# A two-layer hybrid encoder step: the FFN's down projection with the contraction outermost, Strassen operand sums two tiles at a time on VectorE

## The chip, the cores and the metric

One core of a Trainium2 chip. The metric is the device time of one execution in microseconds: the median of the runs, 3462.66 us before the change.

## What is computed

A two-layer encoder step in float32: per layer an RMSNorm, one input projection into four head groups (latent attention, RWKV-7, Mamba-2, gated DeltaNet), an output projection with residual, then RMSNorm and a gated convolutional FFN with residual; a final RMSNorm. The change lies between the output projection and the next layer:

```python
x = x + mix @ P['w_out'][l]
u, new_hist = _dwconv(_rmsnorm(x, g2) @ w_up, hist, conv_w)   # 1024 -> 2 x 2816
gate, val = jnp.split(u, 2, axis=-1)
x = x + (jax.nn.silu(gate) * val) @ w_down                    # 2816 -> 1024
```

The activations lie transposed: 1024 features are eight tiles (`KD`) of 128 partitions, and the 1076 positions (prompt, meta tokens and samples) are three blocks of 308, 384 and 384 columns (`XBLK`). The FFN's 2816 inner features are 22 tiles (`NFF`).

## The kernel before

Every large product is made in a split form: an operand is stored as a rounded high part and the remainder as a low part (`split`, line 277: the high part is a copy on ScalarE, the low part a subtraction on VectorE, or on GpSimd where `pool` is set), and `dense` (line 298) adds three matmuls for each tile of the contraction: high by high, high by low, low by high. `load_w` (line 286) loads a weight tile of up to 1024 columns into one of two raw buffers (`wraw`) and splits it into one of two pairs (`whi`, `wlo`).

The program is written in order of the work, and a scheduler orders each engine's instructions by priority: program order, with the stretches under `high_priority` moved ahead. PSUM has eight buffers of a bank, under tags: two `d`, two `g`, one each of `c`, `h`, `e`, `i` (line 1897). All DMAs are issued by SyncE (`dma`, line 262), in its order.

**Output projection and norm (`w_out`, line 1494).** For each block, eight output tiles `ops` are made, added to the residual tile `xt[b][m]` on VectorE (line 1534) and written to HBM. Then `norm2` squares the eight tiles on ScalarE, adds them up in two accumulators (on VectorE and GpSimd, in block 2 on VectorE alone), sums over the partitions by two matmuls with ones into `nps` (tag `g`, lines 324 to 326) and gets the factor by Ln and Exp. Block 0's and block 1's normed tiles are split into `h0` and `h1` (half of the low parts on GpSimd).

**Strassen operands (lines 1553 to 1575).** Blocks 1 and 2 together go through the up projection as a two by two product with seven products. Its sums of normed tiles are made one 384-column tile at a time: `a11 - a21`, `a22 - a11` and the low parts of S2, S1, S3, S4 on VectorE, the sums `a21 + a22` (line 1567), `a12 - s2` (line 1572) and the low parts of A22 on GpSimd. The seven products of each of the 22 inner tiles (`up12`, line 1658; tile `upq`) need them; block 0 (`up0`, line 1639; tile `ups`) needs only `h0`. `ffn_w` (line 1585) loads two weight tiles, splits them and makes Strassen's four weight sums on GpSimd, in two steps around a `yield`.

**Down projection (lines 1702 to 1744).** The gated tiles lie in HBM (`gd`). `gates(b)` loads a block's 22 tiles as eleven pairs `gr` and splits them into `gh`, `gl` (twelve buffers each). Then each of eight output tiles takes its whole contraction:

```python
for m in range(KD):
    ps = self.pp.tile([P, 512], F32, tag="dg"[m % 2], name=self.nm("wps"))
    for k0 in range(0, NFF, KD):
        kk = min(KD, NFF - k0)
        c = (m % 4 * NFF + k0) * P
        w = self.load_w(io["wdnl"][l, m // 4][:, c:c + kk * P], kk * P)
        self.dense(ps[:, :n], w, xs[k0:k0 + kk], 0, n, 0, k0 == 0, k0 + kk == NFF)
    self.tt(xt[m], xt[m], ps[:, :n], ALU.add)
```

So one output tile needs all 22 gated tiles and three weight tiles (1024, 1024, 768 columns). After the third output tile (`m == 2`) of blocks 1 and 2 the norm of the block before is written (`f(b - 1, prev)`: in layer 0 the next layer's first norm, in layer 1 `out_block`, the final norm and the output). The last block's comes after the loop.

Of the kernel before, what the change touches and what calls it, by code (L numbers as in the profile page):

```python
# [8 lines left out]
F32 = mybir.dt.float32  # L9
# [7 lines left out]
P = 128  # L17
DM = 1024
KD = 8
# [13 lines left out]
NSLOT = 17  # L33
DFF = 2816
NFF = 22
FG = [(0, NFF)]
NF = 5
TI = 800
RB = 0.4
# [159 lines left out]
class Net:  # L199
# [86 lines left out]
    def load_w(self, src, n=1024, act_hi=True, pool=None):  # L286
        raw = self.wp.tile([P, 1024], F32, tag="wraw", name=self.nm("wraw"))
        if pool is None:
            hi = self.wp.tile([P, 1024], F32R, tag="whi", name=self.nm("whi"))
            lo = self.wp.tile([P, 1024], F32R, tag="wlo", name=self.nm("wlo"))  # L290
        else:
            hi = pool.tile([P, 1024], F32R, tag="g", name=self.nm("gwh"))
            lo = pool.tile([P, 1024], F32R, tag="g", name=self.nm("gwl"))
        self.dma(raw[:, :n], src)
        self.split(hi[:, :n], lo[:, :n], raw[:, :n], act_hi)
        return hi, lo

# [14 lines left out]
    def mean_sq(self, xt, n, adds=None):  # L312

        t = lambda tag: self.sp.tile([P, 384], F32, tag=tag, name=self.nm(tag))
        accs = []
        for e in range(2):
            acc = t("na")
            self.act(acc[:, :n], xt[4 * e], AF.Square)
            accs.append(acc)
            for k in range(4 * e + 1, 4 * e + 4):  # L320
                sq = t("nt")
                self.act(sq[:, :n], xt[k], AF.Square)
                (adds or (self.nc.vector, self.nc.gpsimd)[e]).tensor_tensor(acc[:, :n], acc[:, :n], sq[:, :n], op=ALU.add)
        ps = self.pp.tile([P, 512], F32, tag="g", name=self.nm("nps"))
        for e in range(2):
            self.mm(ps[:, :n], self.cc("ones"), accs[e][:, :n], e == 0, e == 1)
        r = accs[0]
        self.rsqrt(r[:, :n], ps[:, :n], 1.0 / DM, 1, accs[1][:, :n])
        return r
# [18 lines left out]
    def norm2(self, xt, b):  # L348

        n = XBLK[b][1]  # L350
        r = self.mean_sq(xt, n, self.nc.vector if b == 2 else None)
# [1134 lines left out]
    def x_block(self, pool, b, src, tag=None):  # L1486

        c0, n = XBLK[b]
        xt = [pool.tile([P, 308 if tag else 384], F32, tag=tag or f"x{k}", name=self.nm("x"))[:, :n] for k in range(KD)]
        for k in range(KD):  # L1490
            self.dma(xt[k], src[k][:, c0:c0 + n])
        return xt

    def w_out(self, l, xdram):

        sa, sb = SIDES[l % 2], SIDES[1 - l % 2]
        xq = self.new("xq", {f"x{k}": 2 for k in range(KD)}, side=sa)
        fq = self.new("fq", dict(x=KD, y=8, g=4), side=sa)
        xt = {}
        for b in [*range(NFB, NBLK), *range(NFB)]:  # L1500
            part = b >= NFB
# [22 lines left out]
        for b in range(NBLK):  # L1524
            c0, n = XBLK[b]
            if b == 2:
                yd[b] = y_last(b)
                ya[b] = self.y_tiles((0,), b)
            for m in range(KD):
                ps = self.pp.tile([P, 512], F32, tag="dei"[m % 3], name=self.nm("ops"))  # L1530
                w = ws[m // 2]
                self.dense(ps[:, :n], w, ya[b], 0, n, m % 2 * 512, True, False)
                self.dense(ps[:, :n], w, yd[b], 0, n, m % 2 * 512 + 256, False, True)
                self.tt(xt[b][m], xt[b][m], ps[:, :n], ALU.add)
                self.dma(self.xres[m][:, c0:c0 + n], xt[b][m])
            if b == 0:
                self.aq.release()
                self.ap.release()
                self.ha = self.new("ha", dict(h0=16, h1=16), side=sb)
                self.h0 = self.pairs(self.ha, 308, KD, "h0")  # L1540
                self.h1 = self.pairs(self.ha, 384, KD, "h1")
            if b == 2:
                with self.tc.high_priority(HPO):
                    self.fw = self.ffn_w(l, 0)
                    next(self.fw)
            scale = self.norm2(xt[b], b)
            if b < 2:
                for k in range(KD):
                    self.split(*(self.h0, self.h1)[b][k], scale(k), pool=k % 2)
        fq.release()  # L1550


        self.hx = self.new("hx", {f"h{i}": 2 * KH for i in range(5)}, side=sb)
        S2, S1, S3, S4, A22 = self.hm = [self.pairs(self.hx, 384, KH, f"h{i}") for i in range(5)]
        sub = lambda o, a, b: self.tt(o, a, b, ALU.subtract)
        K = range(KH)
        a11, a12, a21, a22 = xt[1][:KH], xt[1][KH:], xt[2][:KH], xt[2][KH:]
        s2 = []
        for k in K:
            scale(k)  # L1560
            scale(KH + k)
            sub(a11[k], a11[k], a21[k])
            s2.append(self.sp.tile([P, 388], F32, tag="s", name=self.nm("s2"))[:, :384])
            sub(s2[k], a22[k], a11[k])
            self.split(*S2[k], s2[k])
        for k in K:
            self.nc.gpsimd.tensor_tensor(a21[k], a21[k], a22[k], op=ALU.add)
            self.split(*S1[k], a21[k])
        for k in K:
            self.split(*S3[k], a11[k])  # L1570
        for k in K:
            self.nc.gpsimd.tensor_tensor(a12[k], a12[k], s2[k], op=ALU.subtract)
            self.split(*S4[k], a12[k])
        for k in K:
            self.split(*A22[k], a22[k], pool=True)
        xq.release()
        self.pw.release()

# [6 lines left out]
    def ffn_w(self, l, j):  # L1585

        raws, ws = [], []
        for i in range(2):
# [3 lines left out]
            self.split(*w, raw)  # L1592
            raws.append(raw)
            ws.append(w)
        (B11, B21), (B12, B22) = ((r[:, 0:512], r[:, 512:1024]) for r in raws)
        g = lambda o, a, b, op: self.nc.gpsimd.tensor_tensor(o, a, b, op=op)
        g(B22, B22, B12, ALU.subtract)
# [13 lines left out]
    def ffn(self, l, after):  # L1611
# [27 lines left out]
        def up0(j):  # L1639

            with self.tc.high_priority(HPO):
                w = self.fw if j == 0 else self.ffn_w(l, j)
                W[j] = [x for x in w if x][0]
# [55 lines left out]
        wt.release()  # L1699
        self.hx.release()  # L1700
        self.ha.release()
        xq = self.new("xe", {f"x{k}": 2 for k in range(KD)}, side=sa)
        gq = self.new("gq", dict(gr=3), side=sa)
        ng = 0

        def gates(b):

            nonlocal ng
            c0, n = XBLK[b]
            out = []  # L1710
            for r in range(NFF // 2):
                raw = gq.tile([P, 2, 384], F32, tag="gr", name=self.nm("gr"))[:, :, :n]
                i = ng % 12
                hi, lo = ((gq if i < 8 else xq).tile([P, 2, 384], F32R, tag=f"{s}{i}", name=self.nm(s))[:, :, :n]
                          for s in ("gh", "gl"))
                ng += 1
                self.dma(raw, gd[2 * r:2 * r + 2][:, :, c0:c0 + n].rearrange("j p n -> p j n"))
                self.split(hi, lo, raw)
                out += [(hi[:, i], lo[:, i]) for i in range(2)]
            return out  # L1720

        prev = None
        for b in range(NBLK):
            n = XBLK[b][1]
            with self.tc.high_priority(HPO):
                xs = gates(b)
            xt = self.x_block(xq, b, self.xres)
            for m in range(KD):
                ps = self.pp.tile([P, 512], F32, tag="dg"[m % 2], name=self.nm("wps"))
                for k0 in range(0, NFF, KD):  # L1730
                    kk = min(KD, NFF - k0)
                    c = (m % 4 * NFF + k0) * P
                    w = self.load_w(io["wdnl"][l, m // 4][:, c:c + kk * P], kk * P)
                    self.dense(ps[:, :n], w, xs[k0:k0 + kk], 0, n, 0, k0 == 0, k0 + kk == NFF)
                self.tt(xt[m], xt[m], ps[:, :n], ALU.add)
                if m == 2 and b == 0:
# [198 lines left out]

    def out_block(self, xt, b):
        c0, n = XBLK[b]
        r = self.mean_sq(xt, n)
        for k in range(KD):
            t = self.sp.tile([P, 388], F32, tag="s", name=self.nm("yt"))  # L1940
            self.stt(t[:, :n], xt[k], self.vec("fin", k), r[:, :n], ALU.mult, ALU.mult)
            self.dma(self.io["o_y"][k][:, c0:c0 + n], t[:, :n])


class MultiPool:
# [141 lines left out]
```

## Time and profile before

| | us |
|---|---|
| runs | 3462.30, 3462.66, 3464.98 (median 3462.66) |
| profiled execution | 3456.34 |
| its span | 3454.3 |
| PE busy | 3274.8 (95%) |
| DVE busy | 2393.8 (69%) |
| ACT busy | 1608.3 (47%) |
| POOL busy | 789.4 (23%) |

PE is TensorE, DVE VectorE, ACT ScalarE, POOL GpSimd, SP SyncE. Busy times are sums over stages with different limits; the PE row counts overlapped matmuls, so a stretch is better read by how many matmuls it holds. In layer 0 the output projection and the Strassen operands end near 1000 us, the up projection near 1450 us, the down projection near 1740 us; in layer 1 near 2720, 3152 and 3442 us.

### The profile page before, as it was taken

To read this page: it belongs to the slowest core of one execution; us is meant where nothing else is said; L and a number is where in the kernel's file an instruction comes from. 1 tells how busy PE (TensorE), PEld (TensorE's weight loads), DVE (VectorE), ACT (ScalarE), POOL (GpSimd) and SP (SyncE) were. 2 spreads that over 40 slices of the span, in tenths; PEclk is the share of its full clock that TensorE was granted. 3 is DMA by queue.
4 is the path that set the end of the run, shared out by engine and by line. 5 is a ranking of instruction groups with operands and counts; after the bars stand their busy time and mean duration, and the time that the engine had idled before them with its cause. 6 is when DMAs were issued, how large, how long until landed. Compare 5 with 4: busy or idle time off the path is not lost. (4 is left out here: it accounts for less than half of the span.)

```text
span 3454.3 us, 66279 instructions
## 1 busy us (share of the span) xinstructions
PE 3274.8 (95%) x25954; PEld 2939.2 (85%) x25954; DVE 2393.8 (69%) x4527; ACT 1608.3 (47%) x3285; POOL 789.4 (23%) x1305
## 2 busy tenths in 40 slices
PE   7999999998889999899999999999988999998998
PEld 6988885776879999889998888767768899998998
DVE  5477774774689999845535778657647899996553
ACT  4455555454444444434335555544544444444432
POOL 3000012000255555300020000120004555551000
PEclk9999998999999999999999999989999999999999
DMA  3222223421412222376532232334132222225664
GB/s 133 87 74 78 71 85 100 118 65 49 153 52 75 75 74 74 117 221 190 161 106 72 70 86 70 99 92 124 45 96 94 68 75 75 75 74 171 191 189 128
DMA packets 267417, 350.20 MB, mean 101 GB/s; under 512 B 75424, under 2 KB 225888, under 8 KB 266976
## 3 DMA queue, kind: packets, MB, share of 16 engines
q1 hardware_dynamic: 267104, 345.96, 32.8%
q8 instruction: 204, 3.34, 0.4%
q14 instruction: 109, 0.89, 0.1%
HBM read 256.17 MB, written 89.71 MB: 100 GB/s over the span
## 5 line engine op out<-in xcount | busy, mean ns | idle before, releaser
L283 DVE TENSOR_TENSOR wlo<-wraw,whi 128x1024 fp32r<-128x1024 f32 (+1 forms) x307 | 362.3, 1181 | 306.8 <-ACT whi L280 299.1
L280 ACT CAST whi<-wraw 128x1024 fp32r<-128x1024 f32 (+1 forms) x307 | 311.5, 1015 | 555.9 <-PE wps L239 252.4
L248 DVE SCALAR_TENSOR_TENSOR fct<-frt,vecs,fct 128x384 f32<-128x384 f32 (+1 forms) x528 | 410.9, 822 | 6.1 <-ACT fct L236 4.3
L239 PE MATMUL dps<-hh,whi 128*128 128x384 f32 (+1 forms) x1128 | 391.3, 348 | 12.1 <-ACT hh L280 7.3
L239 PE MATMUL dps<-hl,whi 128*128 128x384 f32 (+1 forms) x1128 | 390.3, 347 | 1.5 <-POOL hl L283 1.1
L239 PE MATMUL dps<-hh,wlo 128*128 128x384 f32 (+1 forms) x1128 | 389.1, 346 | 0.0
L239 PE MATMUL wps<-gh,whi 128*128 128x384 f32 (+1 forms) x1056 | 351.1, 333 | 22.8 <-ACT whi L280 11.5
L239 PE MATMUL wps<-gl,whi 128*128 128x384 f32 (+1 forms) x1056 | 349.0, 331 | 4.5 <-DVE gl L283 4.4
L239 PE MATMUL wps<-gh,wlo 128*128 128x384 f32 (+1 forms) x1056 | 348.7, 331 | 3.6 <-DVE wlo L283 3.4
L239 PE MATMUL upq<-hl,th 128*128 128x384 f32 x704 | 239.4, 340 | 9.7 <-DVE hl L283 9.4
L239 PEld LDWEIGHTS dps<-hh,whi 128*128 128x128 f32 x1128 | 216.8, 193 | 29.9 <-ACT hh L280 10.2
L239 PE MATMUL upq<-hh,th 128*128 128x384 f32 x704 | 239.0, 340 | 2.7 <-ACT hh L280 2.0
L239 PE MATMUL upq<-hh,tl 128*128 128x384 f32 x704 | 238.2, 339 | 3.5 <-DVE tl L283 3.5
L239 PEld LDWEIGHTS dps<-hl,whi 128*128 128x128 f32 x1128 | 217.2, 193 | 16.0 <-issue 6.1
L239 PEld LDWEIGHTS dps<-hh,wlo 128*128 128x128 f32 x1128 | 216.9, 192 | 12.2 <-issue 7.8
L239 PEld LDWEIGHTS wps<-gh,whi 128*128 128x128 f32 x1056 | 202.9, 192 | 27.0 <-ACT gh L280 13.8
L239 PE MATMUL ups<-hh,wlo 128*128 128x308 f32 x704 | 218.6, 311 | 5.1 <-DVE wlo L283 4.3
L239 PE MATMUL ups<-hh,whi 128*128 128x308 f32 x704 | 216.7, 308 | 5.4 <-ACT whi L280 5.4
L239 PE MATMUL ups<-hl,whi 128*128 128x308 f32 x704 | 214.8, 305 | 0.0
L239 PEld LDWEIGHTS wps<-gl,whi 128*128 128x128 f32 x1056 | 202.6, 192 | 8.3 <-DVE gl L283 7.7
L239 PEld LDWEIGHTS wps<-gh,wlo 128*128 128x128 f32 x1056 | 202.5, 192 | 7.6 <-DVE wlo L283 7.3
L239 PE MATMUL upq<-hl,whi 128*128 128x384 f32 x528 | 180.3, 341 | 1.0 <-DVE hl L283 0.6
(418 smaller groups left out, 8042.4 us busy)
## 6 DMA issues: line engine op xcount, KB each, us to landing
wraw<-wdnl SPq DMA_DIRECT2D x96, 512.0 KB, 3.6
wraw<-wup SPq DMA_DIRECT2D x88, 512.0 KB, 4.4
wraw<-win SPq DMA_DIRECT2D x50, 512.0 KB, 4.0
wraw<-wdnl SPq DMA_DIRECT2D x48, 384.0 KB, 3.2
gd<-fct SPq DMA_DIRECT2D x88, 192.0 KB, 1.9
gr<-gd SPq DMA_DIRECT2D x44, 384.0 KB, 4.3
wraw<-wout SPq DMA_DIRECT2D x32, 512.0 KB, 3.7
gd<-fct SPq DMA_DIRECT2D x44, 154.0 KB, 2.0
```

The source lines that it names most:

```text
L239: self.nc.tensor.matmul(out, lhsT, rhs, start=start, stop=stop)
L248: self.nc.vector.scalar_tensor_tensor(out, a, s, b, op0=op0, op1=op1)
L280: self.nc.scalar.copy(hi, src)
L283: (self.nc.gpsimd if pool else self.nc.vector).tensor_tensor(lo, src, hi.bitcast(F32), op=ALU.subtract)
```

## The change

The down projection loops over eleven pairs of contraction tiles outside and over the eight output tiles inside. All eight outputs of a block stay open in PSUM, in all eight banks. A step `r` takes one pair of gated tiles and two weight tiles of 1024 columns (for four outputs and two contraction tiles each), both at high priority; the gated pairs have six buffers. The weights are laid out by step on the host, and a step's tile comes in pieces of 512 columns. `f(b - 1, prev)` comes after step 2.

Residual and normed tiles, `h1` and the Strassen operands are stored two to a tile (`Block`, `Halves`), so that sums and splits work on 768 columns. The sums and low parts that were on GpSimd go to VectorE. `s2` takes tag `nt` (two buffers) in place of `s`. The norm's partial sums are added on VectorE before one matmul with ones; in block 2 of `norm2` and of `out_block` each square goes to its own matmul (`late`), eight in all. The output projection's residual additions get high priority. `ffn_w` has one more `yield`, after the split weights: for tile 1 only that part is at high priority.

```diff
-FG = [(0, NFF)]
+FG = [(2 * i, 2) for i in range(NFF // 2)]
...
     def mean_sq(self, xt, n, late=False):
...
+        if late:
+            for k in range(KD):
+                sq = t("nt")
+                self.act(sq[:, :n], xt[k], AF.Square)
+                self.mm(ps[:, :n], self.cc("ones"), sq[:, :n], k == 0, k == KD - 1)
+        else:
...
+            self.tt(accs[0][:, :n], accs[0][:, :n], accs[1][:, :n], ALU.add)
+            self.mm(ps[:, :n], self.cc("ones"), accs[0][:, :n])
...
-                self.tt(xt[b][m], xt[b][m], ps[:, :n], ALU.add)
+                with self.tc.high_priority(HPO):
+                    self.tt(xt[b][m], xt[b][m], ps[:, :n], ALU.add)
...
+                elif b == 1:
+                    scale(k)
+                    if k % 2:
+                        self.split(*self.h1.pair(k // 2), xt[1].p[k // 2])
...
+        for p in range(H):
+            for i in range(2):
+                scale(2 * p + i)
+                scale(KH + 2 * p + i)
+            sub(a11[p], a11[p], a21[p])
+            for i in range(2):
+                s2 = self.sp.tile([P, 384], F32, tag="nt", name=self.nm("s2"))
+                sub(s2, a22[p][:, i], a11[p][:, i])
+                self.split(*S2[2 * p + i], s2)
+                sub(a12[p][:, i], a12[p][:, i], s2)
+        for p in range(H):
+            self.tt(a21[p], a21[p], a22[p], ALU.add)
+            self.split(*S1.pair(p), a21[p])
+        for S, x in ((S3, a11), (S4, a12), (A22, a22)):
+            for p in range(H):
+                self.split(*S.pair(p), x[p])
...
+            for r in range(nr):
+                with self.tc.high_priority(HPO):
+                    xs = gates(b, r)
+                if r == 0:
+                    xt = self.x_block(xq, b, self.xres)
+                    acc = [self.pp.tile([P, 512], F32, tag=t, name=self.nm("wps"))[:, :n] for t in "ddcheigg"]
+                for h in range(2):
+                    with self.tc.high_priority(HPO):
+                        w = self.load_w(io["wdn2"][l, r, 2 * h:2 * h + 2].rearrange("m p c -> p m c") if r + 1 < nr
+                                        else io["wdnl"][l, h])
+                    for m in range(4 * h, 4 * h + 4):
+                        self.dense(acc[m], w, xs, 0, n, m % 4 * 2 * P, r == 0, r + 1 == nr)
+                        if r + 1 == nr:
+                            with self.tc.high_priority(HPO):
+                                self.tt(xt[m], xt[m], acc[m], ALU.add)
...
-                if m == 2 and b:
+                if r == 2 and b:
                     f(b - 1, prev)
...
-        r = self.mean_sq(xt, n)
+        r = self.mean_sq(xt, n, b == 2)
```

## Rows read from the trace of the kernel before

**Rows 1.** Part 1 of the page: busy time, share, instructions, by engine.
```profile
PE 3274.8 (95%) x25954; PEld 2939.2 (85%) x25954; DVE 2393.8 (69%) x4527; ACT 1608.3 (47%) x3285; POOL 789.4 (23%) x1305
```
**Rows 2.** By stretch: length; busy (x count), PE to POOL; PEclk, DMA share, GB/s.
```profile
925.00:1000.00 75.00, 57.94 (x293) 50.70 (x292) 62.19 (x87) 34.69 (x67) 39.29 (x43) 0.93 0.16 51
...
1450.00:1475.00 25.00, 18.21 (x84) 15.88 (x83) 17.81 (x26) 14.01 (x21) 0.31 (x2) 0.80 0.78 235
1475.00:1500.00 25.00, 19.18 (x125) 18.55 (x124) 8.07 (x9) 7.09 (x9) 0.00 (x0) 0.86 0.76 244
1500.00:1525.00 25.00, 25.00 (x181) 25.00 (x180) 10.74 (x12) 8.63 (x12) 0.00 (x0) 1.00 0.64 179
1600.00:1625.00 25.00, 25.00 (x147) 25.00 (x146) 8.07 (x9) 7.20 (x9) 1.62 (x1) 1.00 0.53 156
1550.00:1750.00 200.00, 194.53 (x1105) 189.62 (x1104) 103.85 (x124) 80.46 (x117) 23.30 (x24) 1.00 0.57 173
2625.00:2725.00 100.00, 83.76 (x424) 75.48 (x423) 82.05 (x116) 45.34 (x87) 51.65 (x59) 0.90 0.17 57
3150.00:3175.00 25.00, 17.98 (x90) 15.71 (x88) 18.29 (x28) 12.54 (x20) 0.87 (x5) 0.86 0.62 187
3175.00:3200.00 25.00, 19.33 (x106) 18.69 (x107) 8.43 (x10) 7.44 (x10) 0.00 (x0) 0.80 0.77 249
...
3250.00:3425.00 175.00, 174.26 (x986) 172.25 (x985) 86.98 (x100) 66.44 (x82) 8.13 (x5) 1.00 0.61 188
```
**Rows 3.** PE's waits, 1440 to 1560 us: total, times, longest.
```profile
PE wps L239 <- ACT whi L280: 5.4, 1, 5.4
PE wps L239 <- ACT gh L280: 5.1, 4, 3.4
```
**Rows 4.** PE's waits, 915 to 1020 us.
```profile
PE ops L239 <- DVE x L242: 4.3, 2, 3.4
PE ups L239 <- ACT whi L280: 3.0, 2, 1.8
```
**Rows 5.** DVE's groups by shape, 950 to 980 us: busy, mean ns, idle.
```profile
L248 DVE SCALAR_TENSOR_TENSOR x<-x,vecs,na 128x384 f32<-128x384 f32 x8 | 7.7, 986 | 2.2 <-ACT na L236 2.2
L283 DVE TENSOR_TENSOR hl<-x,hh 128x384 fp32r<-128x384 f32 x12 | 7.6, 682 | 0.0
L242 DVE TENSOR_TENSOR s<-x,x 128x384 f32<-128x384 f32 x4 | 4.6, 1160 | 0.0
L242 DVE TENSOR_TENSOR x<-x,x 128x384 f32<-128x384 f32 x4 | 3.8, 958 | 0.0
L283 DVE TENSOR_TENSOR hl<-s,hh 128x384 fp32r<-128x384 f32 x4 | 3.0, 745 | 0.0
```
**Rows 6.** POOL's groups by shape, 950 to 980 us.
```profile
L1567 POOL TENSOR_TENSOR x<-x,x 128x384 f32<-128x384 f32 x4 | 5.7, 1424 | 10.5 <-DVE x L242 10.5
```
**Rows 7.** DVE in order of time: start, us, operation.
```profile
1473.09 0.96 DVE L283 TENSOR_TENSOR gl<-gr,gh 128x768 fp32r<-128x768 f32 x1 [0.45 <-ACT gh L280]
...
1561.39 0.55 DVE L242 TENSOR_TENSOR x<-x,wps 128x384 f32<-128x384 f32 x1 [1.29 <-PE wps L239]
```
**Rows 8.** Groups by shape, 1500 to 1545 us.
```profile
L283 DVE TENSOR_TENSOR wlo<-wraw,whi 128x1024 fp32r<-128x1024 f32 x10 | 12.3, 1226 | 12.2 <-ACT whi L280 12.2
L280 ACT CAST whi<-wraw 128x1024 fp32r<-128x1024 f32 x10 | 10.5, 1049 | 18.2 <-PE wps L239 13.5 <-DMA wraw<-wdnl 4.7
```
**Rows 9.** Part 6 of the page: DMA issues, KB each, us to landing.
```profile
wraw<-wdnl SPq DMA_DIRECT2D x96, 512.0 KB, 3.6
...
gr<-gd SPq DMA_DIRECT2D x44, 384.0 KB, 4.3
```
**Rows 10.** PE in order of time, inside the last block of layer 0.
```profile
1678.52 1.45 PE L239 MATMUL nps<-na,const 128*128 128x384 f32 x4
```
**Rows 11.** DVE and SP in order of time, the end of the run.
```profile
3446.92 4.33 DVE L248 SCALAR_TENSOR_TENSOR yt<-x,vecs,na 128x384 f32<-128x384 f32 x8 [3.92 <-ACT na L236]
...
3447.57 4.04 SPq L263 DMA_DIRECT2D o_y<-yt  x8
```

More of the change, by code (lines that the diff above doesn't have):

```diff
@@ L1488, in x_block @@
         c0, n = XBLK[b]
-        xt = [pool.tile([P, 308 if tag else 384], F32, tag=tag or f"x{k}", name=self.nm("x"))[:, :n] for k in range(KD)]
+        xt = Block(pool.tile([P, 2, 308 if tag else 384], F32, tag=tag or f"x{p}", name=self.nm("x"))[:, :, :n]
+                   for p in range(KD // 2))
         for k in range(KD):
@@ L1545, in w_out @@
                     next(self.fw)
+                    next(self.fw)
             scale = self.norm2(xt[b], b)
-            if b < 2:
-                for k in range(KD):
-                    self.split(*(self.h0, self.h1)[b][k], scale(k), pool=k % 2)
+            for k in range(KD):
+                if b == 0:
+                    self.split(*self.h0[k], scale(k), pool=k % 2)
+                elif b == 1:
+                    scale(k)
+                    if k % 2:
+                        self.split(*self.h1.pair(k // 2), xt[1].p[k // 2])
@@ L1558, in w_out @@
[L1558 to L1573, printed above, removed]
@@ L1594, in ffn_w @@
             ws.append(w)
+        yield
         (B11, B21), (B12, B22) = ((r[:, 0:512], r[:, 512:1024]) for r in raws)
@@ L1701, in ffn, with gates @@
         self.ha.release()
-        xq = self.new("xe", {f"x{k}": 2 for k in range(KD)}, side=sa)
+        xq = self.new("xe", {f"x{p}": 2 for p in range(KD // 2)}, side=sa)
         gq = self.new("gq", dict(gr=3), side=sa)
         ng = 0
-        def gates(b):
+        def gates(b, r):
             nonlocal ng
             c0, n = XBLK[b]
[L1710 to L1720, printed above, removed]
+            raw = gq.tile([P, 2, 384], F32, tag="gr", name=self.nm("gr"))[:, :, :n]
+            i = ng % 6
+            hi, lo = ((gq if i < 2 else xq).tile([P, 2, 384], F32R, tag=f"{s}{i}", name=self.nm(s))[:, :, :n]
+                      for s in ("gh", "gl"))
+            ng += 1
+            self.dma(raw, gd[2 * r:2 * r + 2][:, :, c0:c0 + n].rearrange("j p n -> p j n"))
+            self.split(hi, lo, raw)
+            return [(hi[:, i], lo[:, i]) for i in range(2)]
@@ L1722, in ffn @@
         prev = None
+        nr = NFF // 2
         for b in range(NBLK):
             n = XBLK[b][1]
[L1725 to L1736, printed above, removed]
+            for r in range(nr):
[13 more added lines that the diff above has]
+                                self.tt(xt[m], xt[m], acc[m], ALU.add)
+                if r == 2 and b == 0:
@@ L1942, in out_block, with __init__, __getitem__, pair @@
             self.dma(self.io["o_y"][k][:, c0:c0 + n], t[:, :n])
+class Block:
+    def __init__(self, tiles):
+        self.p = list(tiles)
+    def __getitem__(self, k):
+        return self.p[k // 2][:, k % 2]
+class Halves:
+    def __init__(self, hi, lo):
+        self.hi, self.lo = hi, lo
+    def pair(self, p):
+        return self.hi.p[p], self.lo.p[p]
+    def __len__(self):
+        return 2 * len(self.hi.p)
+    def __getitem__(self, k):
+        if isinstance(k, slice):
+            return [self[i] for i in range(*k.indices(len(self)))]
+        if k >= len(self):
+            raise IndexError(k)
+        return self.hi[k], self.lo[k]
 class MultiPool:
```

51 lines of the change are left out of this document (27 added, 24 removed).

## The prediction, made before the changed kernel ran

> **What bounds the kernel now.** I read the page's busy times first, then the stretches around the change, then what PE waits for in them. PE is busy for 95% of the span [rows 1], so time can only come from places where PE stands, runs at the lower clock, or does work that is dropped. A busy share hides the second, so I count matmuls in a stretch [rows 2]. Undisturbed, the down projection issues 181 matmuls of 308 columns in 25 us (0.138 us each) or 147 of 384 columns (0.170 us each). Three places hold fewer:
> - Start of the down projection. Layer 0 has 84 and 125 in its first two stretches of 25 us, 153 too few, or 21.1 us; layer 1 has 90 and 106, 166 too few, or 22.9 us. The granted clock there is 0.80 to 0.86, between the levels of 1.2 and 2.4 GHz, and DMA runs at 187 to 249 GB/s against 154 to 188 later. PE waits for the gated tiles `gh` (5.1 us, 3.4 us of it at once) and once 5.4 us for a weight tile [rows 3].
> - Rest of it. 1550 to 1750 holds 1105 where 1176 would fit, 12.1 us; layer 1's 3250 to 3425 holds 986 of 1029, 7.3 us [rows 2].
> - From the output projection to the up projection. 925 to 1000 holds 293 of 441, 25.2 us; layer 1's 2625 to 2725 424 of 588, 27.9 us. VectorE is busy 62 of 75 us there, GpSimd 39 [rows 2]. PE waits 4.3 us for the residual additions and 3.0 us for the split weights of the up projection [rows 4].
> Together some 116 us, the most that can be won.
>
> **Down projection, start.** Before, the first output tile wants all 22 gated tiles and three weight tiles within 66 matmuls, 9.1 us. After, a step of 48 matmuls (6.6 us at 308 columns, 8.2 us at 384) wants one gated pair and two weight tiles: 2 x 512 KB and 308 or 384 KB, that is 1.36 MB in 6.6 us (206 GB/s) or 1.44 MB in 8.2 us (176 GB/s). Both lie below the 235 to 249 GB/s seen [rows 2]; the second equals the 173 GB/s that blocks 1 and 2 move now. Matmuls, their columns and the bytes of weights stay the same. What stays late is the first pair (3.4 us), about 1 us for its low part, 3 us lost at the lower clock after it (0.80 over 25 us is 10 us at the lower level, 5 us lost, now after two long gaps), and, my estimate from the narrow margin in block 0, 2.5 us for weights behind gated pairs and residual tiles in SP's queue, for SP issues all of them. That keeps 10 of 22 us: **-12 us a layer, -24 us**. Ends: nothing if the first gate delays the whole, -44 us if no gate is late.
>
> **Rest of the down projection.** The next block's gated pairs no longer arrive all at once when one output tile frees them, but one in 8 us. ScalarE's and VectorE's work for a step is 2 x 1.05 and 2 x 1.23 us for weights [rows 8] plus 0.96 us for the pair's low part [rows 7], 3.4 us on VectorE in 8.2. Of 19.4 us I take back a third, **-7 us** (0 to -19). 22 loads of 1024 columns replace 24 mixed ones for each block, hidden under PE. All eight banks are held by a block, so `nps` of the block before, in tag `g`, waits for that block's last outputs: its norm falls beside the next block, which costs nothing in the middle, where VectorE is busy 104 of 200 us [rows 2], and something at the ends (below).
>
> **Strassen operands.** VectorE's 32 operations on single tiles take 7.7 + 7.6 + 4.6 + 3.8 + 3.0 = 26.7 us between 950 and 980 [rows 5], with means of 0.68 to 1.16 us, while GpSimd, which takes 1.42 us for such a sum, works beside it [rows 6]. Alone, VectorE takes 0.55 us for 384 columns and 0.96 us for 768 [rows 7], and 4.33 / 8 = 0.54 us for a scale [rows 11]. After: 8 scales 4.3, two paired subtractions 1.9, four s2, four low parts and four `a12` subtractions 12 x 0.55 = 6.6, two paired sums 1.9, eight paired low parts 7.7: 22.4 us, and no GpSimd. That is 4.3 us shorter. The residual additions go ahead of the other VectorE work, 4.3 us [rows 4]. A shorter gap also saves some clock, which averages 0.93 there: 14% of 75 us at the lower level, 5 us lost; I take 1.5. Against it stands the late norm: `nps` issues four instructions for two matmuls with ones in 1.45 us [rows 10]; eight matmuls are sixteen, 5.8 us, 4.35 more on PE. Net **-6 us a layer, -12 us**. Ends: all 53 us; or nothing, if the up projection's second weight tile, whose raw buffer waits for the same operands, still comes last. `h1`'s low parts move from GpSimd to VectorE, 4 x 0.96 us; products of block 0 cover them, and without that cover they are lost in full, 8 us for both layers. The extra `yield` only moves later weights behind the operands; counted as 0 (within the same ends).
>
> **Norms.** Twelve of the fifteen norms drop one of two matmuls, 12 x 0.72 = 8.7 us of PE, and put one VectorE addition of 0.55 us in front of the other. I take **-4 us** (-9 to +7).
>
> **The ends.** In layer 0 the norm of block 1 now waits until block 2 has ended, where that of block 2 follows. Each is some 7 us of VectorE (8 scales, 4 low parts), against about 15 us of PE work on the next layer's first tiles for blocks 0 and 1 (2 x 24 x 0.14 and 2 x 24 x 0.17): **+3 us** (0 to +8). At the very end two blocks of output remain, not one: 16 scales, 8.7 us for 4.3, and 16 transfers for 8, whose issues now take 4.04 us [rows 11], and the late norm's 5.8 us run beside the first block's scales: **+4 us** (+1 to +8).
>
> **Sum.** -24 - 7 - 12 - 4 + 3 + 4 = -40 us on the profiled execution's 3456.3 us, so 3416. The median of the runs stands 6.3 us above that execution: **3423 us**, 1.2% faster.
>
> **Rivals.**
> - *Each step waits for its weights* (slower). Two raw buffers; each is held for landing, high part and low part: 3.6 us [rows 9] + 1.05 + 1.23 = 5.9 us, so a tile every 2.95 us against 24 matmuls in 3.3 us (308) or 4.1 us (384). At a landing of 6.4 us it is a tile every 4.34 us: 22 x 1.0 + 44 x 0.26 = 33 us a layer, 67 us in all: 3490 us. It decides from a landing of 6.0 us on. For it: gated pairs, which land in smaller pieces, take 4.3 us for 384 KB [rows 9], which scales to 5.7 us for 512 KB, and the new weights come in pieces half as long. Against it: today's loop loads its weights as often and holds 147 matmuls in 25 us at a clock of 1.00 [rows 2]. The Trainium skill's page "TensorE: Matmul & The Clock Gate", section "Loop structure matters more than you think", speaks for this rival: it advises the whole contraction of one output inside the loop, since a load waited for at each step also lowers the clock. The steady rows show no such wait now. Chance 0.06.
> - *Weights partly late*: at a landing of 5.7 us only block 0 suffers, 22 x 0.65 = 14 us a layer: 3423 + 29 = 3452 us. Chance 0.12.
> - *No gate late*: the new gate buffers hold 21 KB a partition against 57, so they may not wait for memory of the up projection, and the start loses 1 us instead of 10: 3423 - 19 = 3404 us. Chance 0.17.
> - *PSUM's full banks*: norms wait and stall PE in its order at every block and both ends, 5 us at each of four places: 3443 us. Chance 0.08.
>
> **Numbers.** The forecast has 0.57. What a measurement of this kernel can tell from no change is 0.2%, 7 us: faster means under 3455.7. Of the second rival I put 0.07 below that bound and 0.05 within it, of the fourth 0.07 and 0.01: faster 0.88, same 0.06, slower 0.06. The range goes from 3390, the forecast less 33 us for more won at the start and at the operands (half of the 20 and the 41 us that the forecast leaves there, and a little), to 3454, beyond the second and the fourth rival.
>
> **What would show it.** Right: the two stretches after the up projection hold over 150 matmuls each, with one wait of some 3 us for the first gate; wps waits below 10 us a layer; 1.36 MB a step at a flat DMA rate; no GpSimd sums between operands, VectorE's means at 0.55 and 0.96 us; one output block more at the end. Wrong: `whi` waits for DMA at each step, a landing over 5.7 us, or 925 to 1000 still holding 293 matmuls because the second weight tile comes last.

## The result, and the profile after

The changed kernel takes 3421.18 us (median of 4 runs, 3418.60 to 3424.20), against 3462.48 us (median of 4) for the kernel before on the same chips: a ratio of 0.9881, with a 95% interval from 0.9864 to 0.9898. That is 41 us, where -40 us and 3423 us were predicted. The profiled execution took 3420.1 us, with a span of 3418.3. One execution of the kernel before on record (4366.78 us, at a granted clock of 0.66) ran in a slower state of the chip and is left out of all ratios.

Executions of one kernel differ by 10 us and more (the twelve of `rest_alone` below range from 3444.62 to 3460.68 us), also in stretches whose code is the same, so the work below is counted inside each trace: from matmul to matmul of a named tile (the 96th `wps`, the 84th `upq`), in the order in which PE ran them. "First 96" runs from the start of the first `wps` to the start of the 97th, so a wait ahead of the 97th counts; stretches behind the last `wps` begin at its end.

| stretch, us | layer 0 before | after | layer 1 before | after |
|---|---|---|---|---|
| last block of the output projection to the 84th `upq` | 71.1 | 65.0 | 71.1 | 66.0 |
| first 96 `wps` | 30.5 | 15.4 | 30.1 | 16.6 |
| the other 1488 `wps` | 255.1 | 246.9 | 253.2 | 250.6 |
| last `wps` to layer 1's 288th `dps` | 51.6 | 59.3 | | |
| last `wps` to the end | | | 11.9 | 16.2 |

The gains are 11.3, 28.6 and 10.8 us, the losses 7.7 and 4.3 us: -38.7. The span fell by 36.0; the 2.7 us between lie in stretches that the change does not touch or that can't be told from the scatter. The first row does not hang on where it is cut: the 168th `upq`, with the same 144 matmuls of `ups` run by then, comes 6.5 and 5.7 us earlier. Five other traces with the same down projection repeat the second row within 1.5 us (15.1 to 15.4 and 15.2 to 16.5), but the third only roughly: 246.9 to 251.3 us in layer 0 and 249.2 to 250.6 in layer 1.

First the page's busy times and the stretches, after (columns as in [rows 2]).

```profile
PE 3268.5 (96%) x25966; PEld 2937.6 (86%) x25966; DVE 2373.0 (69%) x4512; ACT 1601.8 (47%) x3249; POOL 747.9 (22%) x1270
```

```profile
925.00:1000.00 75.00, 63.77 (x324) 55.75 (x323) 58.60 (x88) 36.35 (x60) 28.78 (x32) 0.93 0.17 58
...
1450.00:1475.00 25.00, 25.00 (x168) 24.75 (x167) 15.93 (x20) 12.61 (x16) 0.00 (x0) 0.93 0.86 275
1475.00:1500.00 25.00, 25.00 (x180) 24.96 (x179) 10.99 (x11) 10.19 (x11) 0.00 (x0) 1.00 0.83 280
1500.00:1525.00 25.00, 25.00 (x180) 25.00 (x179) 15.04 (x18) 12.05 (x16) 0.00 (x0) 1.00 0.66 217
...
3150.00:3175.00 25.00, 25.00 (x173) 25.00 (x172) 11.78 (x13) 9.77 (x11) 0.00 (x0) 1.00 0.97 322
3175.00:3200.00 25.00, 25.00 (x172) 25.00 (x171) 11.85 (x11) 9.54 (x10) 0.00 (x0) 1.00 0.67 211
```

The first 50 us of the down projection hold 348 matmuls, where [rows 2] had 209, at a granted clock of 0.93 and 1.00 instead of 0.80 and 0.86. Some 4 us of that difference is the window: the first `wps` starts at 1453.86 us before and at 1449.49 after, and the table counts from there. DMA moves 275 and 280 GB/s in these 50 us, and in layer 1, from 15 to 40 us after its first `wps`, 322; no row of [rows 2] has more than 249. PE's waits from 1440 to 1540 us are down to one, the first gate; the wait of 5.4 us for weights is gone [rows 3]:

```profile
PE wps L239 <- ACT gh L280: 3.4, 1, 3.4
```

At the operands VectorE's shapes from 950 to 980 us answer to [rows 5]. All now take what they take alone, 0.55 to 0.62 us for 384 columns and 0.96 for 768, and from the first scale to the last low part it is 20.4 us instead of 26.4.

```profile
L283 DVE TENSOR_TENSOR hl<-x,hh 128x768 fp32r<-128x768 f32 x8 | 7.1, 955 | 0.0
L248 DVE SCALAR_TENSOR_TENSOR x<-x,vecs,na 128x384 f32<-128x384 f32 x8 | 4.5, 615 | 6.8 <-ACT na L236 6.8
L242 DVE TENSOR_TENSOR x<-x,x 128x768 f32<-128x768 f32 x4 | 3.7, 956 | 0.0
```

But look at the idle time of the second row: 6.8 us in which VectorE waits for the norm's factor, 2.2 in [rows 5]. The late norm on PE, in order of time, shows why: after a wait of 3.45 us, twelve instructions for six of its eight matmuls hold PE for 6.07 us. The granted clock is 0.60 in the first 2.9 us behind that wait and 0.83 in the next 3.2, so part of these 6.07 us is the price of the wait.

```profile
948.63 6.07 PE L239 MATMUL nps<-nt,const 128*128 128x384 f32 x12 [3.45 <-ACT nt L236]
```

At the layer boundary (PE's waits, 1705 to 1770 us) PE now waits for the norms of blocks 1 and 2 one behind the other, and at the end VectorE scales two blocks of output with 2.48 us of idle time between (DVE and SP in order of time; compare [rows 11]).

```profile
PE nps L239 <- DVE na L242: 2.2, 1, 2.2
PE dps L239 <- ACT hh L280: 1.8, 2, 1.4
```

```profile
3403.12 4.33 DVE L248 SCALAR_TENSOR_TENSOR yt<-x,vecs,na 128x384 f32<-128x384 f32 x8 [0.45 <-ACT na L236]
3409.93 4.32 DVE L248 SCALAR_TENSOR_TENSOR yt<-x,vecs,na 128x384 f32<-128x384 f32 x8 [2.48 <-ACT na L236]
...
3403.77 11.00 SPq L263 DMA_DIRECT2D o_y<-yt  x16
```

### The profile page after: what moved, and what is told of

The parts are those of the page before. It is cut to its first block, busy times and chain, and to the rows that moved or that the text cites. A ratio compares the mean times of both kernels' runs of the same rounds, so it can differ in the third digit from the quotient of the medians.

```text
span 3418.3 us, 66168 instructions
## 1 busy us (share of the span) xinstructions
PE 3268.5 (96%) x25966; PEld 2937.6 (86%) x25966; DVE 2373.0 (69%) x4512; ACT 1601.8 (47%) x3249; POOL 747.9 (22%) x1270
## 5 line engine op out<-in xcount | busy, mean ns | idle before, releaser
L283 DVE TENSOR_TENSOR wlo<-wraw,whi 128x1024 fp32r<-128x1024 f32 x295 | 360.7, 1223 | 335.4 <-ACT whi L280 328.1
L280 ACT CAST whi<-wraw 128x1024 fp32r<-128x1024 f32 x295 | 309.5, 1049 | 561.2 <-PE wps L239 265.2
L239 PE MATMUL wps<-gh,whi 128*128 128x384 f32 (+1 forms) x1056 | 343.8, 328 | 6.8 <-ACT gh L280 6.7
L239 PE MATMUL upq<-hh,wlo 128*128 128x384 f32 x528 | 178.4, 338 | 0.0
```

The source lines that it names most:

```text
L239: self.nc.tensor.matmul(out, lhsT, rhs, start=start, stop=stop)
L280: self.nc.scalar.copy(hi, src)
L283: (self.nc.gpsimd if pool else self.nc.vector).tensor_tensor(lo, src, hi.bitcast(F32), op=ALU.subtract)
```

## The experiments

Medians stand against the median of the kernel before on the same chip; a ratio compares the runs of the two, with its 95% interval, and is not the quotient of the medians.

### One half of the change at a time

`down_alone` puts the new loop, its weight layout and its priorities into the kernel before; `rest_alone` puts the old loop into the changed kernel.

> The kernel before with the new down projection alone (contraction outermost, eight banks, streamed gated pairs, weights by step); operands, norms and output projection as before. Theory: the parts add up. In the traces the down projection lost 23 us in layer 0 and 16 us in layer 1, the stretch from it to the next layer's output projection gained 7.5 us and the end of the run about 4 us, of which some belongs to the late norm: -26 to -32 us against before, about 3434 us. The 7.5 us at the layer boundary must be there again. Rival: the down projection gains only because its surroundings changed too (memory freed earlier, norms shorter); then less than -15 us.

Measured: 3436.48 us against 3463.67, ratio 0.9920 (0.9899 to 0.9940), -27 us, as the theory has it. The down projection takes 266.5 and 265.7 us (before 285.5 and 283.3). The boundary stretch takes 57.6 us, 6.0 more than before. The end takes 20.5 us, not 16.2: with two output blocks left, the old form of the norm is slower there than the late one.

> The changed kernel with the old down projection (22 gated tiles at once, one output tile at a time); paired operands on VectorE, the additions at high priority, the new norms and the late norm stay. Theory: -6 to -10 us against before, about 3454 us, all of it between 900 and 1010 us and its like in layer 1; the layer boundary and the end as before within 2 us. Rival: the end of the run grows by the late norm and takes half of it back; then -2 to -5 us.

Measured: 3454.87 us, ratio 0.9972 (0.9958 to 0.9987), -9 us. The stretch to the 84th `upq` takes 65.0 us in both layers, as in after; the boundary 49.4 us. The end takes 14.5 us, 2.6 more than before and not within the 2 us expected: with one output block left, the late norm loses. The product of the two ratios is 0.9892, inside the interval of the whole change. The parts add up.

### Where the down projection's start was won

`gates_at_once` changes the changed kernel's loop so that all pairs of a block are asked for ahead:

```diff
-            for r in range(nr):
-                with self.tc.high_priority(HPO):
-                    xs = gates(b, r)
+            with self.tc.high_priority(HPO):
+                xa = [gates(b, r) for r in range(nr)]
+            for r in range(nr):
+                xs = xa[r]
```

(and twelve buffers as before). `weights_behind` takes `high_priority` off `load_w` in that loop as well.

> The changed kernel with all eleven gated pairs of a block asked for at the block's start and twelve buffers for them, as before the change; contraction outermost and the weights by step as in after. Theory: it is the bunch of gated pairs that cost 22 us a layer at the start, because their 3.4 MB go ahead of the weights in SP's queue; then the first 96 matmuls of wps, 30.5 us before and 15.4 after, take 22 to 30 us again, with PE waiting for weights and not for gates. Rival: the order of the loops alone does it, since step 1 needs one pair whatever else is asked for; then 15 to 18 us.

Measured: 3427.88 us against 3465.99, ratio 0.9891 (0.9849 to 0.9934). The first 96 `wps` take 15.0 and 15.4 us. The theory fell, as far as the pairs go: asking for all of them at once costs nothing at the start, and 1.4 to 2.3 us later (matmuls 96 to 264 take 25.9 and 26.0 us, 23.5 and 24.6 in after).

> The run with all gated pairs asked for at once, and the down projection's weights at normal priority as well, so that SyncE issues pairs and residual tiles ahead of them as before the change; the loops stay contraction outermost. Theory: the loop order won the start (15.0 us for the first 96 matmuls with the pairs at once, 30.5 before) only because the weights' priority let them in between the pairs; behind the pairs they come late, PE waits for whi, and the first 96 matmuls take 22 to 30 us. Rival: the loop order alone does it: 15 to 18 us, for the first weights are issued soon after the first pair in either order.

Measured: 3452.16 us against 3463.45, ratio 0.9965 (0.9951 to 0.9978). The first 96 `wps` take 26.1 and 26.3 us, the down projection 280.3 and 282.1. PE's waits, the first two stretches of 25 us, and SyncE's issues in order of time, of `weights_behind`:

```profile
PE wps L239 <- ACT whi L280: 11.5, 2, 10.7
PE wps L239 <- ACT gh L280: 3.4, 1, 3.4
```

```profile
1447.00:1472.00 25.00, 15.45 (x96) 14.97 (x96) 16.35 (x23) 13.56 (x19) 0.00 (x0) 0.81 0.80 246
1472.00:1497.00 25.00, 22.35 (x133) 21.74 (x134) 10.71 (x10) 9.04 (x9) 0.00 (x0) 0.85 0.82 262
```

```profile
1442.12 9.98 SPq L263 DMA_DIRECT2D gr<-gd  x6
...
1466.90 0.36 SPq L263 DMA_DIRECT2D gr<-gd  x1
1467.31 0.46 SPq L263 DMA_DIRECT2D wraw<-wdn  x1
```

Four weight tiles are issued during the up projection in after and in both of these. The fifth goes out at 1467.31 us here, behind the pairs and behind the residual tiles between them, and at 1457.74 in after. PE stands 10.7 us for it, ahead of the 97th `wps`, and the clock is 0.81 and 0.85 in the two stretches, as low as before the change.

Between `gates_at_once` and `weights_behind` only the priority differs. It is worth 11 us at each start and 14.5 us in each whole down projection (265.8 and 267.6 against 280.3 and 282.1 us), and the ratios lie apart as well, by 0.0074, which is some 26 us. Without it the new loop wins 4 us at each start (30.5 to 26.1 and 30.1 to 26.3), and as a whole execution `weights_behind` can't be told from `rest_alone`, which has the old loop (0.9965 and 0.9972; it does bear the new loop's longer boundary, 58.1 us against 49.4).

That does not make 11 of 15 us the priority's own. The old loop with prioritised weights was not run, but the trace of before bounds what it could win: its first output wants every pair, and the low part of the eleventh is done 18.8 us after the first `wps` in layer 0, with the pairs ahead of all further weights in SyncE's queue (DVE in order of time, before; the second of these two operations is the eleventh pair's):

```profile
1471.13 1.50 DVE L283 TENSOR_TENSOR gl<-gr,gh 128x616 fp32r<-128x616 f32 x2
```

Behind it come some 30 matmuls of 0.14 us, so the 97th could start at some 23 us at the earliest (an estimate from these rows, for pairs that come no sooner), against 30.5 before and 15.4 after. By that, half of the 15 us can't be won without the new order of the loops; and `weights_behind` shows that 11 can't be won without the priority.

### The operands and the norm before them

Four edits of the changed kernel, each of one thing. The table splits the stretch from the first matmul of the output projection's last block to the 84th `upq` (layer 0, us).

| | last residual addition ends | first scale | last low part | 84th `upq` |
|---|---|---|---|---|
| before | 35.4 | 38.8 | 65.3 | 71.1 |
| after | 31.4 | 39.5 | 59.9 | 65.0 |
| `no_prio` | 39.4 | 45.2 | 65.6 | 70.7 |
| `single_operands` | 31.4 | 39.5 | 64.6 | 69.6 |
| `no_late` | 31.3 | 42.0 | 62.3 | 67.4 |
| `h1_pool` | 35.0 | 38.0 | 58.4 | 63.4 |

```diff
-                with self.tc.high_priority(HPO):
-                    self.tt(xt[b][m], xt[b][m], ps[:, :n], ALU.add)
+                self.tt(xt[b][m], xt[b][m], ps[:, :n], ALU.add)
```

> The changed kernel with the output projection's residual additions at normal priority again. Theory: the last block of the output projection takes 33 us instead of 26.6, but the norm behind it starts that much sooner after it, since VectorE has the same work in both; from the block's first matmul to the 84th Strassen matmul (71.1 us before, 65.0 after in layer 0) nothing changes by more than 1.5 us. Rival, the prediction's own term: the priority is worth its 4.3 us of waits in each layer; then this stretch grows by 4 us in both layers.

Measured: 3437.11 us against 3465.99, ratio 0.9924 (0.9896 to 0.9953). The theory fell, and the prediction's term stands: the stretch grows by 5.7 us in layer 0 and 4.8 in layer 1. VectorE's work is the same, as the theory said, but block 1's scales and low parts now go ahead of the additions, and with the PSUM buffers of `ops` full PE stands for one of them (PE's waits from 912 to 962 us, then PE in order of time):

```profile
PE ops L239 <- DVE x L242: 8.4, 1, 8.4
```

```profile
944.36 0.52 PE L239 MATMUL ops<-yl,gwh 128*128 128x384 f32 x1
944.68 0.52 PE L239 MATMUL ops<-yh,gwl 128*128 128x384 f32 x1
...
950.80 0.33 PE L239 MATMUL ops<-yl,gwh 128*128 128x384 f32 x1
950.97 0.33 PE L239 MATMUL ops<-yh,gwl 128*128 128x384 f32 x1
```

Behind the wait a matmul starts every 0.32 us, and only 6 us later every 0.17; the granted clock is 0.50 from 944 to 947 us and 1.00 from 950 to 953. The priority also saves the clock that the wait costs.

`single_operands` puts the code of before, single tiles and GpSimd's sums, in place of the paired loop.

> The changed kernel with the Strassen operands made one tile at a time with the sums and A22's low parts on GpSimd, as before; the residual additions' priority and the late norm stay. Theory: the pairs on VectorE are all that the operands' part gained; from the first scale to the last low part 26 us instead of 20.4, VectorE's operations of 0.55 us at 1.3 us again while GpSimd works, and the stretch to the 84th Strassen matmul 5 to 6 us longer in each layer. Rival: PE is bound there by the up projection's second weight tile, whose raw buffer comes free last; then the operands end later and PE's 84th matmul moves by under 2 us.

Measured: 3428.51 us, ratio 0.9898 (0.9863 to 0.9933). From the first scale to the last low part it is 25.1 us (20.4), and the 84th `upq` comes 4.6 and 3.6 us later, a little less than the theory's 5 to 6 and more than the rival's 2. VectorE's means are back beside GpSimd's (groups by shape, 943 to 972 us):

```profile
L248 DVE SCALAR_TENSOR_TENSOR x<-x,vecs,na 128x384 f32<-128x384 f32 x8 | 7.7, 984 | 6.8 <-ACT na L236 6.8
...
L242 DVE TENSOR_TENSOR s<-x,x 128x384 f32<-128x384 f32 x4 | 4.6, 1158 | 0.0
```

```profile
L1585 POOL TENSOR_TENSOR x<-x,x 128x384 f32<-128x384 f32 x4 | 5.7, 1421 | 14.3 <-DVE x L242 14.3
```

`no_late` drops the `late` branch of `mean_sq` and adds block 2's squares on VectorE:

```diff
-                    (self.nc.vector, self.nc.gpsimd)[e].tensor_tensor(...)
+                    (self.nc.vector if late else (self.nc.vector, self.nc.gpsimd)[e]).tensor_tensor(...)
```

> The changed kernel without the late norm: block 2's squares are added on VectorE again and one matmul with ones sums them, in the FFN's norm and in the final one. Theory: the late norm is what ate half of the operands' gain. In the trace of after PE stands 3.45 us for its squares and then spends 6.1 us on eight matmuls with ones before the scales can start; so 2 to 5 us a layer come back and 1 to 3 us at the end: 5 to 12 us under after. Rival: the squares on ScalarE set the time of the norm either way, and the six additions and one more on VectorE take as long as the matmuls did; then within 3 us of after, or slower.

Measured: 3425.23 us, ratio 0.9900 (0.9874 to 0.9926). The rival holds, and more: the scales start 2.5 us later than in after, the 84th `upq` comes 2.4 and 1.3 us later, and the end takes 20.4 us, 4.2 more. ScalarE, in order of time, shows a cost that I had not thought of:

```profile
945.98 1.28 ACT L236 ACT_TABLE_LOAD   x1
947.54 0.46 ACT L236 ACTIVATE fct<-fct 128x308 f32<-128x308 f32 x1 [0.28 <-DVE fct L248]
948.02 1.28 ACT L236 ACT_TABLE_LOAD   x1
949.32 0.58 ACT L236 ACTIVATE na<-nps,const 128x384 f32<-128x384 f32 x1
...
950.52 1.28 ACT L236 ACT_TABLE_LOAD   x1
951.81 0.53 ACT L236 ACTIVATE na<-na 128x384 f32<-128x384 f32 x1
```

With the sum ready later, PE runs block 0's first up products ahead of the norm, the activation of their gate (`fct<-fct`, the Silu) comes between, and the norm's two activations each load a table again: three loads of 1.28 us. In after the first scale starts 1.2 us after the norm's last matmul, too soon for a load of 1.28. So `no_late` does not price the late norm alone; it prices it against another order of ScalarE.

`h1_pool` adds `pool=True` to the split of `h1`'s pairs.

> The changed kernel with block 1's four paired low parts on GpSimd. In after the last residual addition of block 2 ends 31.4 us after that block's first matmul, though PE starts its last matmul at 26.6. Theory: VectorE's queue holds it back there, with block 1's scales and these low parts of 0.96 us ahead; without them the last addition ends 2 to 3 us earlier and the scales of block 2 start as much earlier (39.5 us after the block's first matmul now), 2 to 6 us for both layers. Rival: GpSimd at work stretches VectorE's operations to 1.3 us, as it did in the operands of before, and gives that back: last addition and scales within 1 us of after or later.

Measured: 3415.91 us against 3463.45, ratio 0.9862 (0.9845 to 0.9879), which overlaps with after. Neither reason held as put. GpSimd does stretch VectorE (a weight tile's low part took 2.87 us in one place, 1.23 in the mean of [rows 8]), and the last residual addition ends 3.7 us later. Yet the scales start 1.5 us earlier: the additions now come further apart, the squares' matmuls run between them, and only 3.0 us lie between the last addition and the first scale, where after has 8.1. The granted clock is 1.00 all through this norm, where after has 0.60 and 0.83: PE's longest wait in it is 1.75 us instead of 3.45.

### The layer boundary

That the norm waits for its bank shows in PE's order. Before, block 0's matmuls with ones run behind the 726th `wps` and block 1's behind the 1254th, well inside the next block. In after they run behind the 1055th and the 1583rd, each ahead of the last matmul of the next block, though both are written after that block's third step.

`norm_early` moves the norm of the block before ahead of the accumulators:

```diff
                 if r == 0:
+                    if b:
+                        f(b - 1, prev)
                     xt = self.x_block(xq, b, self.xres)
...
-                if r == 2 and b:
-                    f(b - 1, prev)
```

> The changed kernel with one move: the norm of the block before is written at the start of a block, before the eight accumulators are taken, and not after step 2; so its one bank of tag g comes free with the old block's outputs and not with the new block's. Theory: the 7.5 us at the layer boundary and the 4 us at the end come from norms that wait a whole block for a bank; both go: -8 to -12 us against after, about 3411 us, and the first weight products of layer 1 start some 6 us sooner after the last wps. Rival: a norm at a block's start takes VectorE, ScalarE and a bank from the first steps, and PE then waits there for weights or the eighth accumulator: the boundary shrinks, but the three blocks of the down projection grow by as much; within 3 us of after.

Measured: 3425.89 us, ratio 0.9887 (0.9865 to 0.9909): no gain. The stretch behind layer 0's last `wps` is back at 51.8 us and the end takes 15.2, 1.0 less than after, as the theory has it in kind; the down projections grew by 7.1 and 4.9 us, as the rival has it, though not for weights. PE's waits in layer 0's down projection, `norm_early`:

```profile
PE nps L239 <- DVE na L242: 4.1, 2, 2.6
PE wps L239 <- DVE wlo L283: 0.6, 1, 0.6
```

The matmul with ones stands 40 and 24 matmuls into blocks 1 and 2, ahead of its operand, and PE takes its work in order. `norm_step3` keeps the bank's place and gives PE 72 matmuls to do first:

```diff
+            k = 3 if b else 1
+            order = [(r, h) for h in range(2) for r in range(k)] + [(r, h) for r in range(k, nr) for h in range(2)]
...
+                    elif b:
+                        f(b - 1, prev)
+                    acc += [self.pp.tile([P, 512], F32, tag=t, name=self.nm("wps"))[:, :n]
+                            for t in "ddcheigg"[4 * h:4 * h + 4]]
```

> The changed kernel with the norm of the block before ahead of the second half of the accumulators, as in the run before it, but in blocks 1 and 2 the first four outputs take steps 0 to 2 before the second four begin, so that 72 matmuls (12 us), not 36, lie between the old block's end and the matmul with ones. Theory: in the run with the early norm the layer boundary shrank by 7.5 us and the block starts grew by 4.1 to 4.8 us each, because PE, in its order, stood 2.6 and 1.5 us for the norm's sums; with 72 matmuls ahead the sums are ready, so matmuls 528 to 576 and 1056 to 1104 of wps take 8.3 to 9 us as in after, the boundary stays at 52 us instead of 59, the end at 15: 8 to 10 us less than after in the sum of these stretches. Rival: the block starts lose the time in any order, because the norm takes ScalarE and VectorE from the weight splits; then these stretches stay above 11 us each, with PE waiting for whi or wlo.

Measured: 3410.94 us against 3465.99, ratio 0.9846 (0.9808 to 0.9884). Matmuls 528 to 576 and 1056 to 1104 take 8.3 to 8.5 us, the boundary 51.8, the end 15.0: 8.7 us less than after in these stretches, as the theory has it. By whole executions alone the two can't be told apart, since the intervals overlap. The first 50 us behind layer 0's last `wps`, after and then `norm_step3`:

```profile
1711.70:1761.70 50.00, 44.34 (x237) 38.62 (x236) 31.03 (x46) 26.73 (x56) 18.91 (x32) 0.97 0.30 98
```

```profile
1711.80:1761.80 50.00, 48.17 (x279) 47.64 (x279) 20.43 (x34) 21.36 (x44) 15.37 (x33) 0.97 0.37 113
```

PE fits 42 matmuls more, because VectorE has one norm there (20.4 us busy) and not two (31.0).

### A version that beats both

`step3_final` is `norm_step3` with `self.mean_sq(xt, n)` in `out_block`, so no late norm at the end. `step3_hybrid` adds, in `mean_sq`'s late branch:

```diff
-                self.mm(ps[:, :n], self.cc("ones"), sq[:, :n], k == 0, k == KD - 1)
+                if k < 5:
+                    self.nc.gpsimd.tensor_tensor(accs[0][:, :n], accs[0][:, :n], sq[:, :n], op=ALU.add)
+                if k == 4:
+                    self.mm(ps[:, :n], self.cc("ones"), accs[0][:, :n], True, False)
+                if k > 4:
+                    self.mm(ps[:, :n], self.cc("ones"), sq[:, :n], False, k == KD - 1)
```

> The run with the norm after three first-half steps, with the last block's final norm summed on VectorE and GpSimd like the others (the FFN's norm keeps the late form). Theory: with one block's outputs left at the end nothing competes for VectorE, and the two accumulators beat eight matmuls with ones, as 11.9 us of tail before against 14.5 in the run with all but the down projection say: tail 12 to 13 us where it was 15.0, so 2 to 3 us less than that run; a candidate that beats both kernels, some 3407 us. Rival: the extra addition on VectorE ahead of the one matmul keeps the tail at 15.

Measured: 3416.14 us against 3463.45, ratio 0.9857 (0.9839 to 0.9875). The end takes 13.1 us, 15.0 without this edit, as the theory has it: the last block's scales start 5.5 us after the last `wps` begins, 7.4 in `norm_step3`. The whole execution missed the 3407 us that were expected, and its interval overlaps with those of after and of `norm_step3`.

> The run before, and in block 2 of the FFN's norm the squares of tiles 0 to 4 are added up on GpSimd, with one matmul with ones for their sum and three for the last three squares. Theory: in after PE takes the eight squares one by one from two buffers, 6.1 us after a wait of 3.45 us, and the scales start 8.2 us after the last residual addition, 3.4 before; with four matmuls the early squares are done by then, and the scales start 3 to 5 us earlier: 5 to 10 us for both layers. Rival: GpSimd's four additions take 1.1 to 1.4 us each and stretch VectorE's residual additions beside them; then the scales start within 1.5 us of 39.5 us after the block's first matmul.

Measured: 3407.06 us against 3463.45, ratio 0.9833 (0.9815 to 0.9852). Its interval lies below that of after, so this version beats both kernels. Against `step3_final` the scales start 1.9 us earlier in both layers, between theory and rival, and the 84th `upq` comes 0.8 and 1.8 us earlier: GpSimd's additions make the last residual addition 2.5 us later, and the norm behind it takes 3.7 us instead of 8.1. DVE in order of time, `step3_hybrid`:

```profile
948.42 0.54 DVE L242 TENSOR_TENSOR x<-x,ops 128x384 f32<-128x384 f32 x1
...
952.70 2.21 DVE L248 SCALAR_TENSOR_TENSOR x<-x,vecs,na 128x384 f32<-128x384 f32 x4 [2.35 <-ACT na L236]
```

Against `step3_final` and `norm_step3` the intervals overlap, so the timing alone does not settle this last step.

## Why the prediction came out right, and where it did not

- **Down start, predicted -24, measured -28.6.** The sign and the place were right, the reason only in part. The prediction counted what a step wants, one pair and two weight tiles, and left the priority of the weight loads without a price, though it is part of the change. `weights_behind` keeps what a step wants and loses 11 of layer 0's 15 us, so counting bytes for a step does not carry the term. Of the 10 us that were to stay lost, the 3.4 us for the first pair stayed. The 3 us at the lower clock measured some 1.5 in layer 0: from 1451.3 to 1454.4 us a matmul starts every 0.256 us, before and behind that every 0.140. The 2.5 us "for weights behind gated pairs and residual tiles in SP's queue" were nothing with the priority (no wait for `whi` in either layer) and 11 us without it.
- **Rest of the down projection, predicted -7, measured -10.8** (8.2 and 2.6). This was a guess, a third of a shortfall, and came out inside its ends. In layer 0 PE's waits for weights and gated tiles fall from 4.8 to 1.0 us there; for the rest no cause is shown, and part of it is scatter.
- **Operands, predicted -12, measured -11.3.** By its own terms, in layer 0: the residual additions -4.3, measured -4.1 to the last of them; the sequence on VectorE -4.3, measured -6.1; the late norm +4.35, measured +4.8 between the last addition and the first scale; clock and rest -1.5, measured -0.8. Two of these need a word. The sequence after takes 20.4 us where 22.4 were added up, because the records of neighbouring operations overlap: seven paired low parts take 6.17 us together, 0.88 each and not 0.96. And the 4.8 us are not the price of sixteen instructions on PE: with the same eight matmuls that distance is 3.0 us in `h1_pool`, and without them 10.6 in `no_late`. In the rows of after that distance is filled by the wait of 3.45 us for squares and by six matmuls at the lower clock behind it.
- **Norms, predicted -4.** Not to be told from the scatter of the stretches in which they lie.
- **Layer boundary, predicted +3, measured +7.7.** The mechanism was right (block 1's norm waits for a bank until block 2 has ended), the cover too generous: the next layer's first products do not hide the second norm's work on VectorE (31.0 us busy in the 50 us, 20.4 with one norm). The other traces with this boundary have 57.6 to 59.5 us, so the loss is 6 to 8 us.
- **End, predicted +4, measured +4.3.** The sum was right, but the late norm, counted as a cost, is a gain there while two blocks are left (16.2 against 20.4 in `no_late`) and a cost of some 2 us once one is left.
- **The rivals.** Weights that are late at each step did not show: landing is 3.8 us (it had to be 6.0), and in both down projections PE waits 1.0 us in all for split weights (`wlo`), and never for `whi`. The Trainium skill's page "TensorE: Matmul & The Clock Gate", section "Loop structure matters more than you think", advises against a load waited for at each step. No load is waited for at each step here, and behind the start the granted clock is 1.00 with the contraction outermost; where `weights_behind` does wait, 10.7 us at once, the clock falls to 0.81, which agrees with the page. PSUM's full banks did cost time, at the layer boundary and at the end, not at every block.

```profile
wraw<-wdn SPq DMA_DIRECT2D x120, 512.0 KB, 3.8
...
gr<-gd SPq DMA_DIRECT2D x44, 384.0 KB, 4.1
```

What stays open: how much of the 15 us the old loop with prioritised weights would have won (by the estimate above, at most half), and what the extra `yield` does; neither was tried alone.

## What to carry to other kernels

When several streams share one issuing queue, price the order in that queue as a term of its own: here the new order of the loops was worth little (4 us at each start) until the weight loads went ahead in that queue, and then 15. When a block holds all of PSUM's banks, place each small matmul that needs one so that its bank comes free early and its operand is ready when PE's order reaches it; both had to hold before the boundary's time came back. Compare stretches inside traces by counted matmuls, since whole executions scatter by more than such a step is worth.

## What the runs showed of the hardware that I had not expected

- Reordering alone can bring in ScalarE table loads: three of 1.28 us each around one norm in `no_late`, when the gate's activation fell before the norm's Ln and Exp.
- A wait of PE cost more than its length here: behind the 3.45 us in the norm the granted clock was 0.60 and then 0.83, behind the 8.4 us in `no_prio` 0.50 (the lower level, 1.2 GHz) for 3 us.
- With GpSimd at work beside it, VectorE took 0.98 us in the mean for a 384-column scale, 0.62 alone, and more for single operations: 2.87 us for a 1024-column low part in `h1_pool`, 1.63 us for one scale in `step3_hybrid`.
- In the down projection DMA moved 275 and 280 GB/s in layer 0's first 50 us and 322 in 25 us of layer 1, against 249 at most in the rows read before.
